# First stage of a hybrid decoder layer on one core: scale row, order of the first loads, and products on zeros

## The chip, the core and the metric

One core of a Trainium2 chip runs the whole kernel in one launch. The metric is the device time of an execution in microseconds (us), from the first to the last instruction; below, the median of three runs. Engines are called by their names: TensorE (products and transposes; PE in the profile, PEld its weight loads), VectorE (DVE), ScalarE (ACT), GpSimd (POOL), and SyncE (SP), which only issues transfers.

## What is computed

The reference is one decoder layer for 512 tokens of width 1024 in float32: a gated feed-forward block of inner width 2816, a mixer (four differential attention heads beside state-space channel groups), and a second feed-forward block. Each is normed before and after. Only the beginning matters here:

```python
def rms_norm(x, g):
    xf = x.astype(jnp.float32)
    y = xf * lax.rsqrt(jnp.mean(xf * xf, axis=-1, keepdims=True) + EPS)
    return (y * g.astype(jnp.float32)).astype(x.dtype)

def swiglu(x, w_gate, w_up, w_down):
    return (jax.nn.silu(x @ w_gate) * (x @ w_up)) @ w_down
...
h = swiglu(rms_norm(x, ff1_pre_g[l]), ff1_w_gate[l], ff1_w_up[l], ff1_w_down[l])
```

## The kernel before

**Tiling.** The 512 tokens are four blocks of 128 (`x_sb[0]` to `x_sb[3]`, L101). A block stands with its tokens on the partitions and its 1024 values along them. `load_x` (L103) fetches a block on SyncE's queue, blocks 0 and 1 in two halves each (L109, L110).

**Norm.** `Normed.tile(t)` (L176) norms a block in two halves of 512 columns. `sum_sq` (L164) has ACT square a half; the sum goes to one column, and the squares themselves, which nobody reads, to a tile called junk, one for the norms in front of a block and one for those behind (L96, L166). `rsqrt_of` (L155) adds the two sums on VectorE (L158) and takes the root on GpSimd (L161). VectorE then multiplies each half by that column and by the scale row (L185). The scale row has to stand on all 128 partitions: `gain_row` (L112) lets GpSimd's queue load it 128 times from memory (L115). TensorE transposes the scaled halves (L190), ACT writes their high part (L193), rounded to the products' number format, and VectorE the rest as a low part (L194).

**Products.** A product of two float32 matrices is three products of high and low parts (`mm3`, L149). `weights` (L136) loads 512 KB of weights on SyncE's queue into one of three raw buffers (L137, L138); ACT writes their high part (L125) and VectorE or GpSimd the low part (L126). The first feed-forward block begins with four such column units, two of w_gate and two of w_up (L994 to L1000): first for the tokens of blocks 0 and 1, which are normed first, then for blocks 2 and 3 (`halves`, L212). Its very first unit takes the low part of the weights last (L216 to L221). After that a column unit is 24 products of 512 columns, and parameter work for the state-space part is drawn in between them (`tick`).

**Order.** The engines' queues aren't written by hand in this stage. A scheduler takes the instructions in the program's order, but lets a later one go ahead on its engine where an earlier one isn't ready; each engine then runs its list in order. A buffer is written again only when its readers are done, and the scheduler adds the waits. What is held by hand is a few instructions that are issued behind others (`after`, `behind`): the parts of the first weights behind the high and low parts of the first tokens (L995), and the squares of blocks 2 and 3 behind those of blocks 0 and 1 (L999).

The layer begins so:

```python
    xn = Normed(ff1_pre_g)
    started = [xn.tile(t) for t in range(NT)]
    for g in started[0:2]:
        next(g)
...
        behind[:] = [normed[0 if n == 0 else 1], normed[2]]
        lead1.append(col_weights(w, f * P))
        if n < 2:
            load_x(2 + n)
            with after(*normed[1:]):
                next(started[n])
```

Of the kernel before, what the change touches and what calls it, by code (L numbers as in the profile page):

```python
# [8 lines left out]
F32 = mybir.dt.float32  # L9
# [7 lines left out]
P = 128  # L17
# [32 lines left out]
def hybrid_layer(  # L50
# [24 lines left out]
    def claim(tl):  # L75
        """Takes the page now, before its first real writer is due."""
        pool.memset(tl[:, 0, 0, 0:1] if len(tl.shape) == 4 else tl[:, 0, 0:1], 0.0)
        return tl
# [7 lines left out]
    def bank(tag="m", name="bank"):  # L86
        return psum.tile([P, 512], F32, tag=tag, name=name, bufs=4 if tag == "acc" else 2)

    # ------------------------------------------------------------------ constants
# [6 lines left out]
    junk = {tag: const.tile([P, 512], BF16, name=f"junk_{tag}") for tag in ("pre", "post")}  # L96
    mhalf = const.tile([P, 1], F32, name="mhalf")
    pool.memset(mhalf, -0.5)

    # ------------------------------------------------------------------ residual stream  # L100
# [8 lines left out]
    load_x(0, 2)  # L109
    load_x(1, 2)  # L110

# [8 lines left out]
    # ------------------------------------------------------------------ exact float32 products  # L120
# [7 lines left out]
    @contextmanager  # L128
    def after(*instructions):
        """What this block puts on the engines of these instructions is issued behind them."""  # L130
        with ExitStack() as order:
            for ins in instructions:
                order.enter_context(tc.issue_after(ins))
            yield

    def weights(src, shape, paged=False):  # L136
        raw = ring.tile(shape, F32, tag="raw", name="raw", bufs=3)  # L137
        sp.dma_start(out=raw, in_=src)  # L138
        if paged:
            both = page([P, 2] + list(shape[1:]), F32R, "w_lead")  # L140
            wh, wl = both[:, 0], both[:, 1]
        else:
            wh = ring.tile(shape, F32R, tag="wh", name="wh")
            wl = ring.tile(shape, F32R, tag="wl", name="wl")
        with after(*behind):
            split(raw, wh, wl, pool if paged else lo_engine[0])
        return wh, wl
# [6 lines left out]
    # ------------------------------------------------------------------ norms  # L154
# [9 lines left out]
    def sum_sq(src, scale, tag):  # L164
        s = tiny(1, f"ss_{tag}", bufs=4)
        into = junk["pre" if tag[:3] == "pre" else "post"][:, 0:src.shape[1]]  # L166
        sum_sq.ins = act.activation(into, src, AF.Square, scale=scale, accum_out=s).ins  # L167
        return s

    class Normed:  # L170
        def __init__(self, gain):
            self.g = gain_row(gain, DM, "pre_g")
            self.hi = [page([P, 4, SEQ], F32R, "xn_hi") for _ in range(2)]
            self.lo = [page([P, 4, SEQ], F32R, "xn_lo") for _ in range(2)]
# [25 lines left out]
    # ------------------------------------------------------------------ projections  # L200
    def col_weights(w, c0, paged=False):
        return weights(w[0, :, c0:c0 + P].rearrange("(k p) c -> p k c", p=P), [P, KD, P], paged)
# [9 lines left out]
    def halves(units, xn, started, late_lo=False):  # L212
        """Four column units, first for the tokens that are normed first."""
        for a in (0, 256):
            for j, (ps, (hi, lo)) in enumerate(units):
                if late_lo and a == j == 0:  # L216
                    for k in range(KD):
                        for n in range(2):
                            pe.matmul(ps[:, 0:256], hi[:, k, :], xn.get(k, 0, 256)[n], start=(k == n == 0), stop=False)
                    for k in range(KD):  # L220
                        pe.matmul(ps[:, 0:256], lo[:, k, :], xn.get(k, 0, 256)[0], start=False, stop=(k == KD - 1))  # L221
                else:
                    col_mm(ps, (hi, lo), xn, a, a + 256)
                if a == 0 and j in (0, 2) and started:
                    for _ in started.pop(0):
                        pass

    def outer(nf, last, ts=range(NT)):
        """Reduction-outer order, the last steps token block by token block."""
        return [(f, t) for f in range(nf - last) for t in ts] + [(f, t) for t in ts for f in range(nf - last, nf)]  # L230
# [69 lines left out]
    # ------------------------------------------------------------------ SwiGLU  # L300
# [39 lines left out]
    # ------------------------------------------------------------------ float32 functions on short rows  # L340
# [92 lines left out]
    # ------------------------------------------------------------------ state-space parameters  # L433
    def cmul_rows(o, a, b):
        """o, a, b: [P, 2, GP] complex rows."""
        t = row(2 * GP).rearrange("p (r g) -> p r g", r=2)
        u = row(2 * GP).rearrange("p (r g) -> p r g", r=2)
        dve.tensor_tensor(t, a, b[:, 0:1, :].broadcast_to([P, 2, GP]), ALU.mult)
        dve.tensor_tensor(u, a, b[:, 1:2, :].broadcast_to([P, 2, GP]), ALU.mult)
        dve.tensor_tensor(o[:, 0, :], t[:, 0, :], u[:, 1, :], ALU.subtract)  # L440
        dve.tensor_tensor(o[:, 1, :], t[:, 1, :], u[:, 0, :], ALU.add)

    def cmul_wide(o_re, o_im, a_re, a_im, f, g0, ng, inner):
        """o = a * f for [P, ng, inner] tiles and per-(partition, group pair) factors f [P, 2, GP]."""
# [17 lines left out]
    def pslot(shape, dtype=F32, name=""):  # L462
        """Next 2 KB slot of the pages that the parameter work owns."""
# [18 lines left out]
    def ssm_small():  # L482
# [50 lines left out]
        # (a_bar - 1) / lam  # L533
# [16 lines left out]
        # skip gains of four groups, on partitions 32 apart, and where they stand among the taps  # L550
# [7 lines left out]
    def ssm_tables():  # L558
        # phases of e^{i theta 8 c}
# [17 lines left out]
        # input and output maps  # L577
# [36 lines left out]
    def ssm_maps(blk):  # L614
        if True:
# [3 lines left out]
            # a^{7-tau} b_bar, transposed to rows (tau, h')  # L619
# [19 lines left out]
            # C a^{t+1}  # L639
# [14 lines left out]
            # C a^j for j = 0 to 8  # L654
# [8 lines left out]
            # Re(C a^j b_bar) and the skip, the rows of the causal block matrix  # L663
# [45 lines left out]
    # ------------------------------------------------------------------ state-space mixer  # L709
# [119 lines left out]
    # ------------------------------------------------------------------ differential attention  # L829
# [17 lines left out]
    def att_query(h, xn):  # L847
        """Scaled queries of the two components, [hi; lo] and [lo; hi] on the partitions."""
# [9 lines left out]
    def att_key(h, xn):  # L858
        """Keys: the high part of each component on both halves, the low parts as they come."""
# [47 lines left out]
    def att_norm(h, i):  # L907
        """One token block of a head's output, normed; yields before the transposes back."""
# [24 lines left out]
    def merged(*streams):  # L933
        """Streams of (length, generator), each kept equally far along."""
# [47 lines left out]
    # ------------------------------------------------------------------ the layer  # L982
    xn = Normed(ff1_pre_g)
# [10 lines left out]
    for n, (f, w) in enumerate((f, w) for f in range(2) for w in (ff1_w_gate, ff1_w_up)):  # L994
        behind[:] = [normed[0 if n == 0 else 1], normed[2]]  # L995
        lead1.append(col_weights(w, f * P))
# [131 lines left out]
```

## Time and profile before

| | |
|---|---|
| three runs, us | 987.87, 988.95, 989.09 |
| median, us | 988.95 |
| span of the profiled execution, us | 988.80 |
| TensorE busy, products | 956.1 us, 97% |
| VectorE, ACT, GpSimd busy | 471.4, 339.4, 157.3 us |
| bytes moved | 107.70 MB, 109 GB/s on the mean |
| granted TensorE clock, mean | 0.990 |

The span of the profiled execution runs from its first to its last instruction. No other time of that execution is given, so it stands for its own time; it is 0.15 us below the median. TensorE is busy nearly always, so its idle time and its clock are what is left. The column of the granted clock has records only from TensorE's first rise on: in the first 20 us it reads 1.00 although the products there run at about half the later pace, so for that stretch the pace itself is to be read.

### The profile page before, as it was taken

To read this page: it belongs to the slowest core of one execution; us is meant where nothing else is said; L and a number is where in the kernel's file an instruction comes from. 1 tells how busy PE (TensorE), PEld (TensorE's weight loads), DVE (VectorE), ACT (ScalarE), POOL (GpSimd) and SP (SyncE) were. 2 spreads that over 40 slices of the span, in tenths; PEclk is the share of its full clock that TensorE was granted. 3 is DMA by queue.
4 is the path that set the end of the run, shared out by engine and by line. 5 is a ranking of instruction groups with operands and counts; after the bars stand their busy time and mean duration, and the time that the engine had idled before them with its cause. 6 is when DMAs were issued, how large, how long until landed. Compare 5 with 4: busy or idle time off the path is not lost.

```text
span 988.8 us, 12741 instructions
## 1 busy us (share of the span) xinstructions
PE 956.1 (97%) x4931; PEld 791.5 (80%) x4931; DVE 471.4 (48%) x946; ACT 339.4 (34%) x567; POOL 157.3 (16%) x216
## 2 busy tenths in 40 slices
PE   5999999999999999998899899999999999999997
PEld 4988777788888888986677677988888888888886
DVE  5599877633331325447467657623333333322323
ACT  5423333323221334222577545522223232312221
POOL 2105333100000033236234315000000000000000
PEclk9999999999999999999899899999999999999999
DMA  7535543533323261596211205322333333232312
GB/s 226 166 92 153 163 131 109 152 97 95 107 86 107 86 192 50 212 195 141 65 43 43 86 23 169 107 64 86 107 87 104 93 99 104 88 107 85 107 43 86
DMA packets 146172, 107.70 MB, mean 109 GB/s; under 512 B 15568, under 2 KB 126704, under 8 KB 145344
## 3 DMA queue, kind: packets, MB, share of 16 engines
q1 hardware_dynamic: 143776, 100.93, 34.8%
q0 software_dynamic: 1184, 3.87, 1.4%
q10 hardware_dynamic: 1152, 2.10, 0.6%
q8 instruction: 39, 0.64, 0.3%
q14 instruction: 21, 0.17, 0.1%
HBM read 97.99 MB, written 8.88 MB: 108 GB/s over the span
## 4 chain that ended last, share of the span: by engine, by line
PE 48%; ACT 1%; DVE 1%; issue 1%; DMA 1%; POOL 0%; DVEq 0%; POOLq 0%; ACTq 0%
PE ps_gu L152 8%; PE ps_gu L150 8%; PE ps_gu L151 8%; PE acc L152 5%; PE acc L150 5%; PE acc L151 5%; PE ps_sc L879 1%; PE ps_o L904 1%; PE ps_sc L878 1%; PE ps_y L776 1%; PE ps_k L150 1%; PE ps_sc L880 1%; DMA raw<-in_ff_w_gate_dram 1%; PE ps_k L151 0%; PE ps_q L150 0%
## 5 line engine op out<-in xcount | busy, mean ns | idle before, releaser
L125 ACT CAST wh<-raw 128x1024 fp32r<-128x1024 f32 x150 | 157.7, 1053 | 448.5 <-issue 152.9
L126 DVE TENSOR_TENSOR wl<-raw,wh 128x1024 fp32r<-128x1024 f32 x132 | 164.1, 1246 | 249.2 <-ACT wh L125 245.1
L150 PE MATMUL ps_gu<-xn_hi,wh 128*128 128x512 f32 (+1 forms) x696 | 265.3, 382 | 0.0
L151 PE MATMUL ps_gu<-xn_lo,wh 128*128 128x512 f32 (+1 forms) x696 | 265.2, 381 | 0.0
L152 PE MATMUL ps_gu<-xn_hi,wl 128*128 128x512 f32 (+1 forms) x696 | 264.9, 381 | 0.0
L150 PEld LDWEIGHTS ps_gu<-xn_hi,wh 128*128 128x128 f32 x696 | 130.8, 188 | 25.4 <-issue 0.8
L152 PEld LDWEIGHTS ps_gu<-xn_hi,wl 128*128 128x128 f32 x696 | 130.8, 188 | 25.0
L151 PEld LDWEIGHTS ps_gu<-xn_lo,wh 128*128 128x128 f32 x696 | 131.0, 188 | 24.7
L150 PE MATMUL acc<-wh,h 128*128 128x512 f32 x352 | 136.9, 389 | 0.0
L151 PE MATMUL acc<-wl,h 128*128 128x512 f32 x352 | 136.9, 389 | 0.0
L152 PE MATMUL acc<-wh,h 128*128 128x512 f32 x352 | 136.1, 389 | 0.0
L319 DVE TENSOR_TENSOR hf<-sg,ps_gu 128x512 f32<-128x512 f32 x44 | 30.2, 686 | 105.8 <-PE ps_gu L152 105.1
L150 PEld LDWEIGHTS acc<-wh,h 128*128 128x128 f32 x352 | 66.1, 188 | 13.8
L152 PEld LDWEIGHTS acc<-wh,h 128*128 128x128 f32 x352 | 66.1, 188 | 13.6
L151 PEld LDWEIGHTS acc<-wl,h 128*128 128x128 f32 x352 | 66.1, 188 | 13.6
L281 POOL TENSOR_SCALAR ss<-ss_post 128x1 f32<-128x1 f32 x12 | 2.6, 213 | 457.8 <-ACT junk_post L167 457.8
L126 POOL TENSOR_TENSOR wl<-raw,wh 128x1024 fp32r<-128x1024 f32 x18 | 44.1, 2456 | 52.8 <-ACT wh L125 52.7
L321 ACT CAST h<-hf 128x512 fp32r<-128x512 f32 x44 | 27.3, 621 | 36.6 <-DVE hf L319 30.0
L322 DVE TENSOR_TENSOR h<-hf,h 128x512 fp32r<-128x512 f32 x44 | 30.1, 684 | 1.4 <-ACT h L321 1.4
L190 PE MATMUL ps_xn<-ident,xs 128*128 128x128 f32 x96 | 14.9, 299 | 13.7 <-DVE xs L185 12.1
L167 ACT ACTIVATE junk_post<-acc 128x512 bf16<-128x512 f32 x24 | 14.3, 596 | 40.1 <-PE acc L152 39.9
L317 ACT ACTIVATE sg<-ps_gu 128x512 f32<-128x512 f32 x44 | 25.8, 587 | 1.5 <-PE ps_gu L152 1.5
(283 smaller groups left out, 1220.4 us busy)
## 6 DMA issues: line engine op xcount, KB each, us to landing
raw<-in_ff_w_gate_dram SPq DMA_DIRECT2D x44, 512.0 KB, 3.9
raw<-in_ff_w_up_dram SPq DMA_DIRECT2D x44, 512.0 KB, 3.9
raw<-in_ff_w_down_dram SPq DMA_DIRECT2D x44, 512.0 KB, 3.3
raw<-in_w_in_dram SPq DMA_DIRECT2D x16, 512.0 KB, 4.1
raw<-in_w_out_dram SPq DMA_DIRECT2D x8, 512.0 KB, 3.3
im_d<-itca SPq DMA_DIRECT2D x4, 512.0 KB, 5.0
om_d<-taps SPq DMA_DIRECT2D x4, 512.0 KB, 3.7
im<-im_d SPq DMA_DIRECT2D x2, 1024.0 KB, 10.2
```

The source lines that it names most:

```text
L125: act.copy(wh, raw)
L126: eng.tensor_tensor(wl, raw, wh.bitcast(F32), ALU.subtract)
L150: pe.matmul(ps, a[0], b[0], start=start, stop=False)
L151: pe.matmul(ps, a[0], b[1], start=False, stop=False)
L152: pe.matmul(ps, a[1], b[0], start=False, stop=stop)
L167: sum_sq.ins = act.activation(into, src, AF.Square, scale=scale, accum_out=s).ins
L190: pe.transpose(ps[:, k * P:(k + 1) * P], xs[h][:, k * P:(k + 1) * P], ident)
L317: act.activation(sg, ps_g, AF.Silu)
L319: dve.tensor_tensor(hf, sg, ps_u, ALU.mult)
L321: act.copy(hi, hf)
L322: dve.tensor_tensor(lo, hf, hi.bitcast(F32), ALU.subtract)
L776: pe.matmul(ps[par * 64:par * 64 + 64, g * 64:(g + 1) * 64], lhs, rhs[:, g, par], start=(g == n == 0), stop=(g == 7 and n == 1), skip_grou ...
```

## The change

- The scale row of the first norm is loaded once, 4 KB into one partition on ACT's queue, and spread over the 128 partitions by two float32 products with a row of ones, whose results ACT copies into the row's tile (half by half).
- The two junk tiles become one. It is set to zero by VectorE, and TensorE begins with 14 products of 128x512 that read this tile for both operands.
- The first and second load of weights wait: a one-column copy on GpSimd writes into their raw buffer, and reads the last column of token block 0 and of block 1. The third and fourth have no such copy.
- Comments and docstrings go.

```diff
-    junk = {tag: const.tile([P, 512], BF16, name=f"junk_{tag}") for tag in ("pre", "post")}
+    junk = const.tile([P, 512], BF16, name="junk")
+    dve.memset(junk, 0.0)
...
+    ones = const.tile([1, P], F32, name="ones")
+    dve.memset(ones, 1.0)
+
+    def warm(n):
+
+        ps = bank(name="ps_warm")
+        for _ in range(n):
+            pe.matmul(ps, junk[:, 0:P], junk, start=True, stop=True)
...
     load_x(0, 2)
+    first_g = gains.tile([P, DM], F32, tag="gain", name="pre_g")
+    act.dma_start(out=first_g[0:1, :], in_=ff1_pre_g[0:1, :])
     load_x(1, 2)
+    warm(14)
+    for h in range(2):
+        cs = slice(h * 512, (h + 1) * 512)
+        ps = bank("acc", "ps_g")
+        pe.matmul(ps, ones, first_g[0:1, cs], start=True, stop=True)
+        act.copy(first_g[:, cs], ps)
...
-    def weights(src, shape, paged=False):
+    def weights(src, shape, paged=False, behind_x=None):
         raw = ring.tile(shape, F32, tag="raw", name="raw", bufs=3)
+        if behind_x is not None:
+            pool.tensor_copy(raw[:, 0, 0:1], behind_x)
         sp.dma_start(out=raw, in_=src)
...
-        into = junk["pre" if tag[:3] == "pre" else "post"][:, 0:src.shape[1]]
+        into = junk[:, 0:src.shape[1]]
...
-        def __init__(self, gain):
-            self.g = gain_row(gain, DM, "pre_g")
+        def __init__(self, gain, g=None):
+            self.g = g if g is not None else gain_row(gain, DM, "pre_g")
...
-    def col_weights(w, c0, paged=False):
-        return weights(w[0, :, c0:c0 + P].rearrange("(k p) c -> p k c", p=P), [P, KD, P], paged)
+    def col_weights(w, c0, paged=False, behind_x=None):
+        return weights(w[0, :, c0:c0 + P].rearrange("(k p) c -> p k c", p=P), [P, KD, P], paged, behind_x)
...
-    xn = Normed(ff1_pre_g)
+    xn = Normed(ff1_pre_g, first_g)
...
-        lead1.append(col_weights(w, f * P))
+        lead1.append(col_weights(w, f * P, behind_x=(x_sb[0][:, DM - 1:DM], x_sb[1][:, DM - 1:DM], None, None)[n]))
```

## Rows read from the trace of the kernel before

**Rows 1.** The page: busy time and share of each engine

```profile
PE 956.1 (97%) x4931; PEld 791.5 (80%) x4931; DVE 471.4 (48%) x946; ACT 339.4 (34%) x567; POOL 157.3 (16%) x216
```

**Rows 2.** Waits of TensorE, 0 to 100 us: us in total, times, longest

```profile
PE ps_xn L190 <- DVE xs L185: 11.4, 2, 10.2
```

**Rows 3.** Windows: length, busy PE, PEld, DVE, ACT, POOL; PEclk, DMA, GB/s

```profile
80.00:100.00 20.00, 20.00 (x92) 16.55 (x91) 19.60 (x53) 5.82 (x7) 9.95 (x16) 1.00 0.65 178
```

**Rows 4.** Timeline, 0 to 25 us: start, us, engine, line, what [idle before]

```profile
0.72 1.28 ACT L167 ACT_TABLE_LOAD   x1 [0.72 <-PEq L1114]
...
3.77 0.63 ACT L167 ACTIVATE junk_pre<-x 128x512 bf16<-128x512 f32 x1 [1.77 <-DMA x<-in_x_dram]
...
5.73 0.56 POOL L161 TENSOR_TENSOR rinv_pre<-rinv_pre,mhalf 128x1 f32<-128x1 f32 x1 [2.30 <-DVE rinv_pre L158]
...
9.37 1.42 DVE L185 SCALAR_TENSOR_TENSOR xs<-x,rinv_pre,pre_g 128x512 f32<-128x512 f32 x2 [3.73 <-DMA pre_g<-in_ff_pre_g_dram]
...
10.95 0.63 ACT L167 ACTIVATE junk_pre<-x 128x512 bf16<-128x512 f32 x1 [1.06 <-DMA x<-in_x_dram]
...
11.48 0.19 ACT L167 ACTIVATION_READ_ACCUMULATOR junk_pre<-x 128x1 f32 x1
...
12.59 1.42 DVE L185 SCALAR_TENSOR_TENSOR xs<-x,rinv_pre,pre_g 128x512 f32<-128x512 f32 x2 [0.67 <-POOL rinv_pre L161]
12.67 1.05 ACT L125 CAST wh<-raw 128x1024 fp32r<-128x1024 f32 x1
...
13.92 1.28 DVE L194 TENSOR_TENSOR xn_lo<-ps_xn,xn_hi 128x512 fp32r<-128x512 f32 x2
...
15.25 1.46 DVE L194 TENSOR_TENSOR xn_lo<-ps_xn,xn_hi 128x512 fp32r<-128x512 f32 x2
...
15.99 0.58 PE L219 MATMUL ps_gu<-xn_lo,wh 128*128 128x256 f32 x1 [0.23 <-DVE xn_lo L194]
```

**Rows 5.** Groups by form on GpSimd: count, busy us, mean ns

```profile
L98 POOL MEMSET mhalf<- 128x1 f32 x1 | 0.1, 98 | 0.0
```

**Rows 6.** Windows of the start; the last two are DMA share, GB/s

```profile
1.50:4.50 3.00, 0.00 (x0) 0.00 (x0) 0.22 (x1) 1.22 (x3) 1.91 (x6) 1.00 0.80 242
...
8.50:11.00 2.50, 0.82 (x4) 0.82 (x5) 1.42 (x2) 0.78 (x3) 0.00 (x0) 1.00 0.94 308
```

**Rows 7.** Timeline of TensorE, 458 to 482 us

```profile
462.33 0.35 PE L878 MATMUL ps_sc<-k,q 128*128 128x256 f32 x1 [3.16 <-DVE tsin L746]
...
477.15 0.63 PE L152 MATMUL ps_q<-xn_hi,wl 128*128 128x512 f32 x1
477.58 0.63 PE L150 MATMUL ps_q<-xn_hi,wh 128*128 128x512 f32 x1
```

**Rows 8.** Timeline of TensorE, 0 to 20 us

```profile
19.35 0.37 PE L150 MATMUL ps_gu<-xn_hi,wh 128*128 128x256 f32 x1
19.56 0.28 PE L151 MATMUL ps_gu<-xn_lo,wh 128*128 128x256 f32 x1
19.68 0.52 PE L221 MATMUL ps_gu<-xn_hi,wl 128*128 128x256 f32 x3
```

**Rows 9.** Timeline of TensorE, 505 to 507.5 us

```profile
505.87 0.83 PE L904 MATMUL ps_o<-v,att 128*128 128x128 f32 x6
```

**Rows 10.** Groups by form on ACT

```profile
L839 ACT COPY v<-acc 128x512 f32<-128x512 f32 x4 | 2.1, 600 | 0.0
```

**Rows 11.** Windows of TensorE: length, busy us, PEclk, DMA, GB/s

```profile
462.00:463.00 1.00, 0.67 (x4) 1.00 0.36 106
...
464.00:465.00 1.00, 1.00 (x15) 0.50 0.00 0
```

**Rows 12.** Timeline of SyncE's issues, 5 to 60 us

```profile
11.43 2.62 SPq L487 DMA_DIRECT2D ldt<-in_ssm_log_dt_dram  x1
14.18 1.76 SPq L554 DMA_DIRECT2D dcol<-in_ssm_d_dram  x4
17.90 0.39 SPq L138 DMA_DIRECT2D raw<-in_ff_w_up_dram  x1
```

## Prediction

> **What bounds the kernel now.** I read the page's busy shares first: TensorE is busy for 97% of the span [rows 1], so time can be won only where it idles or runs at its lower clock. Then its waits in the first 100 us: nearly all of its idle time there, 11.4 us, is two waits of the first transposes (L190) for the normed tokens (L185), the longest 10.2 us [rows 2]. From then on its stream has no hole for a long while (20.00 us busy of 20.00 [rows 3]). Weights, scalings and parameter work behind the start are released by TensorE's own progress through rings of buffers, so I take it that an earlier start moves all of that forward, one for one. The figure to forecast is the moment the product stream becomes steady, 15.99 us [rows 4].
>
> The timeline of the first 16 us shows why it is 15.99 [rows 4]. Engines start at 0.72. The squares of token block 0 start at 3.77, its root ends at 6.29 (5.73 + 0.56), yet its scaling starts only at 9.37: it waits for the scale row that GpSimd loads as 128 copies. That isn't the last wait. The second half of block 1 lands at 10.95; squares, sum and root take until its scaling at 12.59, 1.64 us later. From there to 15.99 are 3.40 us, on VectorE mainly: two scalings (1.42), two low parts of block 0 (1.28 from 13.92), two of block 1 (from 15.25). So the late landing of block 1 sets the start; the scale row alone is hidden behind it.
>
> **The change, part by part.** *Scale row.* 512 KB from the GpSimd queue go away, 4 KB on ACT's queue come; ACT issues it ahead of any square and the 4 KB have until about 6.7 us to land. *Weights behind tokens.* Two one-column copies on GpSimd, about 0.1 us each (nearest: a 128x1 memset, 98 ns [rows 5]), wait for blocks 0 and 1. Behind them on GpSimd stands the root of block 0, due later than both, so they cost nothing there. Without the 512 KB, blocks 0 and 1 (1.05 MB) are the first bytes: 0.73 MB have moved by 4.50 at 242 GB/s, the remaining 0.32 MB take 1.0 to 1.3 us at 308 to 242 GB/s [rows 6], so block 1 lands near 5.8 instead of 10.95, 5.1 us earlier. This cover falls away, and what is late next counts.
>
> *Products on zeros.* This is what is late next. The diff makes one tile, junk, of the two that the squares write to (L166), and the 14 products read that tile. So the first square cannot write before the last zero product has read. Call its end T. A memset of 128x512 on VectorE is not in the trace: 0.1 us (a one-column memset [rows 5]) to 0.71 (one scaling [rows 4]); I take 0.3, near the lower end since it reads nothing, and 0.1 of hand-over: TensorE starts at 1.1. A 512-column product takes 0.43 us at the 1.2 GHz level (477.15 to 477.58) [rows 7], so 14 take 6.0, and with the last one's tail (0.63 - 0.43) T = 7.3. Before, the pitch of 256-column products fell from 0.21 to 0.12 us at 19.56 [rows 8], 3.57 us after the stream became steady. If the zeros do as much, 8 run slowly (3.4 us) and 6 at about 0.22, and T = 6.1. I take the middle, T = 6.7; with the memset's bounds, 5.9 to 7.7.
>
> *Behind T.* ACT computes two squares of block 0; each with its sum takes 0.72 us (10.95 to 11.48 + 0.19 [rows 4]), two about 1.5. The two scale products are float32: a record pair of 128 columns is 0.22 us (six records in 0.83 with the tail, so 0.11 apart) [rows 9], times four for 512 columns, 0.9 us each at 2.4 GHz and about 1.75 at 1.2. At 2.4 they are ready at T+0.9 and T+1.8, and ACT copies each in 0.60 [rows 10]: T+1.5 to T+2.7. Then the squares of block 1, 1.5, to T+4.2; sum and root 0.95 (11.67 to 12.59 before, 0.92). Its scaling starts at T+5.15 = 11.85, against 12.59. Block 0's scaling, at T+2.5, is out of the way. The 3.40 us behind it remain, being VectorE's: the stream is steady at 15.25, 0.74 us earlier.
>
> *Clock.* I count nothing for it behind T. Between the scale products (end near 8.5) and 15.25 TensorE has only sixteen transposes, in two bursts. Later in this kernel a wait of 3.16 us, up to 462.33 [rows 7], is followed by a granted clock of 0.50 (1.2 GHz) at 464 us [rows 11]; here two waits of about two us surround one burst. So the stream probably begins at 1.2 GHz, as before, and pays the same.
>
> *First weights.* SyncE's queue isn't written by hand: before, a small parameter load (ldt) was issued at 11.43, ahead of the fourth weights (17.90), which stand earlier in the program but had to wait [rows 12]. So while the first weights wait for GpSimd's copy, blocks 2 and 3 and the third weights (no copy before them) can go ahead. Up to and with the first weights that is 3.2 MB at most: 2.4 MB after 4.50, at 308 GB/s 7.9 us, so 12.4 [rows 6]. Their high part (1.05 us, [rows 4]) is then there at 13.5, before the stream's 15.25: hidden, with 1.8 us to spare. The second weights, 0.52 MB more, land near 14.1 and are wanted 24 products later: hidden.
>
> **Sum.** 15.99 - 15.25 = 0.74 us less: 988.80 (the profiled span; no other time of that execution is given) becomes 988.06. The span stands 0.15 below the median of the runs, 988.95, so I predict 988.2. Bounds of T alone give 987.4 to 989.2. I take 0.2% (2.0 us) as about what a measurement of this kernel tells from no change; the forecast lies inside.
>
> **Rivals.** *The clock holds (faster).* If TensorE is still at 2.4 GHz at the steady start, 17 products of 256 columns save 0.21 - 0.12 us each [rows 8], 1.6 us; the time is 988.2 - 1.6 = 986.6, and 986.0 if T is 6.1. For it: the transposes keep TensorE partly busy. Against it: the fall at 464 [rows 11]. The Trainium skill (TensorE: Matmul & The Clock Gate, "What's actually happening") speaks for it: the slow clock is the default and "activity releases the throttle", so zeros should do it too; its section "HAM oscillation" speaks against its lasting, since there a wait between bursts brings the slow clock back. Chance 0.28, an unforeseen better order on ACT included.
>
> *The first weights come late (slower).* ACT runs in order, and the high part of the first weights stood ahead of block 1's high parts (12.67 [rows 4]). If they land at G, the stream can start no sooner than G + 1.05 + 0.60 + 0.7 = G + 2.35 (weights' high part, one cast, one low part). That decides from G = 12.9, is slower than before from 13.6 and by over 0.2% from 15.6. At 242 GB/s the 2.4 MB last until 14.4, and the tiny loads (ldt, and dcol, 1.76 us to issue at 14.18 [rows 12]) may go ahead too: G = 16, start 18.35, 991.3. For it: the order of [rows 12]; against: 308 GB/s and more were reached. The Trainium skill (DMA: Bandwidth & Descriptors, "HWDGE ordering") says that each DMA engine takes a queue's descriptors in ring order; by this the weights asked for last do come last, which would make it likelier, and no row here tests it. Chance 0.18.
>
> *Zeros do not lift the clock (no change).* Then T = 7.3, the scale products end at T+3.5, the last copy at T+4.1, block 1's scaling is at T+6.55 = 13.85 and the stream at 17.25: 1.26 us later, 990.2. Chance 0.08.
>
> **Numbers.** Forecast 0.46, clock 0.28, late weights 0.18, idle zeros 0.08. So faster 0.28, same 0.46 + 0.08 = 0.54, slower 0.18. The forecast's own range is 987.4 to 989.2; the range for 8 in 10 goes to the fast end of the clock case, 985.9, and past the idle zeros into the late weights, 990.9.
>
> **What would show it.** Right: the first square starts at the end of the zero products, near 6.7, though block 0 has landed before 5; block 1's scaling near 11.9; the steady stream near 15.3 with 0.21 us between products at first. Wrong: squares that start at 3.8 (no wait on junk: the start then moves by some 3 us and the forecast fails on the fast side); products 0.12 us apart from the start (clock); ACT waiting for the weights' load ahead of block 1's high parts (late weights); or a TensorE hole behind 20 us that wasn't there.

## The result, and the profile after

The changed kernel takes 995.03 us (median of five runs, 993.0 to 995.36); the kernel before takes 988.95 (five runs of the same chip, 987.87 to 992.15). The ratio is 1.0056, 95% interval 1.0038 to 1.0074: **slower by 0.56%**, where 988.2 and no change were forecast. The profiled execution has a span of 993.2 us and a time of 995.03, so 1.8 us lie outside the span; that was so in every later run with both numbers. So a span doesn't stand for a time: the profiled execution of before, with its span of 988.80, took about 990.6 us (an estimate by the same 1.8), which is 1.6 above its median and not 0.15 below it. The two profiles lie 4.45 us apart and the medians 6.1 (the ratio, over all runs, is 5.5 us); what the profiles below explain is the 4.45. Line numbers are now 19 higher than before.

The page's first part, after; [rows 1] answer to it. TensorE has 18 records more (the 14 products on zeros and the scale row's two products, four records), and is just as full:

```profile
PE 962.9 (97%) x4949; PEld 794.6 (80%) x4949; DVE 470.8 (47%) x948; ACT 341.2 (34%) x569; POOL 158.3 (16%) x217
```

TensorE's waits over the whole span, after (in all, times, longest). Of the first line's 5.4 us, 4.5 lie in the start (two waits, 3.3 and 1.2), where before it were 11.4 [rows 2]: TensorE is busy with zeros for much of the rest. The second line has grown from 0.2 us.

```profile
PE ps_xn L209 <- DVE xs L204: 5.4, 3, 3.3
PE ps_u L169 <- ACT xn_hi L212: 4.3, 1, 4.3
...
PE ps_it L654 <- DVE itca L469: 1.8, 1, 1.8
PE ps_warm L107 <- DVE junk L97: 1.2, 1, 1.2
```

The line that answers to the second, in the same list of before:

```profile
PE ps_u L150 <- ACT xn_hi L193: 0.2, 1, 0.2
```

Where the time goes can be read from the start of the first product of each stage in both timelines (us, one profiled execution each):

| first product of | before | after | later by |
|---|---|---|---|
| the first column units (ps_gu) | 15.18 | 16.61 | 1.43 |
| the 27th product of them | 20.64 | 21.16 | 0.52 |
| the 1001st (parameter work lies before it) | 237.72 | 238.97 | 1.25 |
| the mixer's first projection (ps_u) | 393.66 | 399.31 | 5.65 |
| attention's products with the values (ps_o) | 486.11 | 492.02 | 5.91 |
| attention's output (o_att) | 575.78 | 580.11 | 4.33 |
| end of the last instruction | 988.80 | 993.25 | 4.45 |

So the start costs half a microsecond, and **4.4 us are lost at one place, 380 us behind everything that the change edits on purpose**: between the first feed-forward block and the mixer.

**The start.** Timeline of the changed kernel, 0 to 20 us (start, us, engine, line, what, idle before and its releaser); [rows 4] answer to it:

```profile
1.18 5.25 PE L107 MATMUL ps_warm<-junk 128*128 128x512 bf16 x14 [1.18 <-DVE junk L97]
...
6.46 0.63 ACT L186 ACTIVATE junk<-x 128x512 bf16<-128x512 f32 x1 [1.57 <-PE ps_warm L107]
...
9.07 0.23 DVE L863 TENSOR_SCALAR subln<-subln 128x128 f32<-128x128 f32 x1 [7.34 <-DMA subln<-in_attn_subln_g_dram]
9.22 0.21 DVE L177 TENSOR_SCALAR rinv_pre<-ss_pre,ss_pre 128x1 f32<-128x1 f32 x1
9.48 0.63 ACT L186 ACTIVATE junk<-x 128x512 bf16<-128x512 f32 x1 [1.07 <-DMA x<-in_x_dram]
...
10.10 0.18 POOL L156 COPY raw<-x 128x1 f32<-128x1 f32 x1 [5.51 <-DMA x<-in_x_dram]
...
10.24 0.56 POOL L180 TENSOR_TENSOR rinv_pre<-rinv_pre,mhalf 128x1 f32<-128x1 f32 x1
...
10.84 1.41 DVE L204 SCALAR_TENSOR_TENSOR xs<-x,rinv_pre,pre_g 128x512 f32<-128x512 f32 x2 [1.42 <-POOL rinv_pre L180]
...
13.42 0.69 DVE L213 TENSOR_TENSOR xn_lo<-ps_xn,xn_hi 128x512 fp32r<-128x512 f32 x1 [1.04 <-ACT xn_hi L212]
...
14.03 1.40 DVE L204 SCALAR_TENSOR_TENSOR xs<-x,rinv_pre,pre_g 128x512 f32<-128x512 f32 x2
14.41 1.05 ACT L142 CAST wh<-raw 128x1024 fp32r<-128x1024 f32 x1 [0.18 <-DMA raw<-in_ff_w_gate_dram]
...
17.34 0.58 PE L238 MATMUL ps_gu<-xn_lo,wh 128*128 128x256 f32 x1
```

The first square waits for the last product on zeros (6.46). Block 1 lands at 9.5 and 10.1 (its square, and GpSimd's copy that reads its last column). VectorE stands for 7.34 us at the scaling of a small row for attention, subln, whose load is late; block 0's sum stands behind it. GpSimd stands for block 1 at its second copy, and block 0's root behind that. So block 0 is scaled at 10.84 instead of 9.37, block 1 at 14.03 instead of 12.59, behind a low part of block 0, and the stream is steady at 17.34 instead of 15.99.

Windows of the same stretch (length; busy PE, PEld, DVE, ACT, POOL; PEclk, DMA share, GB/s): between 4.5 and 6.5 us the transfers fall to less than half of what they are on either side (113 GB/s), with no 512 KB of copies in the way any more. And the clock is down in the last row; it had risen during the zeros, whose last four stand 0.22 us apart and the others 0.43.

```profile
1.50:4.50 3.00, 3.00 (x8) 1.06 (x7) 0.23 (x1) 0.89 (x1) 1.39 (x5) 1.00 0.87 237
4.50:6.50 2.00, 2.00 (x8) 0.74 (x7) 0.00 (x0) 0.43 (x2) 0.09 (x1) 1.00 0.69 113
6.50:8.50 2.00, 1.83 (x4) 0.51 (x4) 0.00 (x0) 1.88 (x5) 0.00 (x0) 1.00 0.74 265
8.50:11.00 2.50, 0.00 (x0) 0.00 (x0) 0.51 (x3) 1.52 (x4) 0.71 (x2) 0.56 1.03 375
```

**The mixer's doorstep.** Here the first block's result is normed and added to the residual x (squares of acc, junk_post before), and the new x is normed for the mixer (squares of x, junk_pre before). ACT's timeline, before, 378 to 402 us:

```profile
380.71 0.63 ACT L167 ACTIVATE junk_pre<-x 128x512 bf16<-128x512 f32 x1 [1.79 <-DVE x L288]
...
381.34 0.58 ACT L167 ACTIVATE junk_post<-acc 128x512 bf16<-128x512 f32 x1
...
381.91 0.62 ACT L167 ACTIVATE junk_pre<-x 128x512 bf16<-128x512 f32 x1
...
386.62 0.60 ACT L167 ACTIVATE junk_post<-acc 128x512 bf16<-128x512 f32 x1 [1.37 <-PE acc L152]
```

The same view, after:

```profile
382.01 0.63 ACT L186 ACTIVATE junk<-x 128x512 bf16<-128x512 f32 x1 [1.85 <-DVE x L307]
...
382.77 0.63 ACT L186 ACTIVATE junk<-x 128x512 bf16<-128x512 f32 x1
...
383.52 0.60 ACT L186 ACTIVATE junk<-acc 128x512 bf16<-128x512 f32 x1
...
388.64 0.60 ACT L186 ACTIVATE junk<-acc 128x512 bf16<-128x512 f32 x1
...
396.51 0.63 ACT L186 ACTIVATE junk<-x 128x512 bf16<-128x512 f32 x1 [3.98 <-DVE x L307]
```

Before, the square of the next acc stands *between* the two squares of x: the two write different tiles, so the scheduler may swap them. After, all write one tile, each is ordered behind the one ahead of it in the program, and the square of acc stands behind both. It comes 2.2 us later than before (383.52 against 381.34), of which 1.2 are the whole kernel's lag and 0.9 the order's. VectorE's list changes with it. Before, the sum of block 1's new x (L288, 382.92) stood ahead of block 0's scalings (384.25); after, it stands behind them (386.30 against 384.97), so block 1's scalings start at 390.09 instead of 386.44. VectorE's timeline, before:

```profile
382.92 0.75 DVE L288 SCALAR_TENSOR_TENSOR x<-half,rinv_post,x 128x512 f32<-128x512 f32 x1
...
384.25 1.41 DVE L185 SCALAR_TENSOR_TENSOR xs<-x,rinv_pre,pre_g 128x512 f32<-128x512 f32 x2
...
386.44 1.41 DVE L185 SCALAR_TENSOR_TENSOR xs<-x,rinv_pre,pre_g 128x512 f32<-128x512 f32 x2 [0.66 <-POOL rinv_pre L161]
...
388.64 0.75 DVE L288 SCALAR_TENSOR_TENSOR x<-half,rinv_post,x 128x512 f32<-128x512 f32 x1
```

The same view, after. At 390 us the scalings meet something:

```profile
384.97 1.41 DVE L204 SCALAR_TENSOR_TENSOR xs<-x,rinv_pre,pre_g 128x512 f32<-128x512 f32 x2
386.30 0.75 DVE L307 SCALAR_TENSOR_TENSOR x<-half,rinv_post,x 128x512 f32<-128x512 f32 x1
...
390.09 3.56 DVE L204 SCALAR_TENSOR_TENSOR xs<-x,rinv_pre,pre_g 128x512 f32<-128x512 f32 x2
393.57 2.84 DVE L307 SCALAR_TENSOR_TENSOR x<-half,rinv_post,x 128x512 f32<-128x512 f32 x1
```

and in GpSimd's, after and then before:

```profile
390.35 5.52 POOL L143 TENSOR_TENSOR wl<-raw,wh 128x1024 fp32r<-128x1024 f32 x2
```

```profile
389.11 4.91 POOL L126 TENSOR_TENSOR wl<-raw,wh 128x1024 fp32r<-128x1024 f32 x2 [0.50 <-ACT wh L125]
```

Two scalings take 3.56 us instead of 1.41, and the step behind them, which makes block 2's new x (L307), 2.84 instead of 0.75: both now fall beside GpSimd's low parts of the mixer's weights. By the trace's single records, which the line merges, the first of the two scalings, which began before the low parts, took 0.74 us; the second took 2.90, so it and the step behind it were each held by 2.1 to 2.2 us, together the size of TensorE's wait. Before, block 2's x was done at 390.06, 0.95 us after those had begun (389.11). ACT waits 3.98 us for that x, and TensorE 4.27 for an ACT that stands there. That GpSimd's low parts are what holds the two is read from these times; no run took them out of the way. TensorE's timeline, after:

```profile
399.31 1.01 PE L169 MATMUL ps_u<-xn_hi,w_lead 128*128 128x256 f32 x3 [4.27 <-ACT xn_hi L212]
```

The windows show the second price of such a hole: the granted clock falls behind it. After:

```profile
395.00:400.00 5.00, 0.73 (x4) 0.69 (x3) 4.19 (x7) 3.49 (x9) 2.63 (x2) 0.79 0.51 175
400.00:405.00 5.00, 5.00 (x26) 4.99 (x26) 4.06 (x8) 1.77 (x5) 1.63 (x3) 0.53 0.35 108
```

Before, for the same ten microseconds:

```profile
395.00:400.00 5.00, 3.93 (x34) 3.69 (x32) 5.00 (x2) 1.72 (x3) 4.53 (x2) 1.00 1.02 414
400.00:405.00 5.00, 4.54 (x38) 4.57 (x39) 3.86 (x8) 2.04 (x5) 0.56 (x2) 1.00 1.00 403
```

The projections then take as long as before (27.1 us from the first to the last ps_u in both), since before they had waits of their own; so the loss is the wait, 4.3 of the 4.4 us. Of the 5.9 us at 486 us, 1.6 come back in attention: before has two stretches at half clock there, near 552 and 562 us, after only one, near 558.

### The profile page after: what moved, and what is told of

Same layout as the page of the kernel before. It is cut to its first block, busy times and chain, and to the rows that moved or that the text cites. A ratio compares the mean times of both kernels' runs of the same rounds, so it can differ in the third digit from the quotient of the medians.

```text
span 993.2 us, 12798 instructions
## 1 busy us (share of the span) xinstructions
PE 962.9 (97%) x4949; PEld 794.6 (80%) x4949; DVE 470.8 (47%) x948; ACT 341.2 (34%) x569; POOL 158.3 (16%) x217
## 4 chain that ended last, share of the span: by engine, by line
PE 48%; DVE 2%; ACT 1%; POOL 1%; issue 1%; DMA 1%; POOLq 0%; DVEq 0%; ACTq 0%
PE ps_gu L170 8%; PE ps_gu L171 8%; PE ps_gu L169 8%; PE acc L169 5%; PE acc L170 5%; PE acc L171 5%; PE ps_sc L898 1%; PE ps_o L923 1%; PE ps_y L795 1%; PE ps_sc L897 1%; PE ps_k L169 1%; DMA raw<-in_ff_w_gate_dram 1%; PE ps_sc L899 1%; PE ps_k L170 0%; PE ps_q L169 0%
## 5 line engine op out<-in xcount | busy, mean ns | idle before, releaser
L186 ACT ACTIVATE junk<-acc 128x512 bf16<-128x512 f32 x24 | 14.3, 597 | 38.8 <-PE acc L171 38.5
L902 ACT ACTIVATE att<-ps_sc,mx 128x128 f32<-128x128 f32 (+3 forms) x32 | 16.8, 526 | 19.8 <-DVE mx L901 19.3
```

The lines of the kernel that those rows point to most:

```text
L902: act.activation(pg[:, c, 0:n], ps[:, 0:n], AF.Exp, bias=mx, accum_out=ssum[:, c:c + 1])
```

## The experiments

Theory A: one junk tile for all squares fixes their order on ACT, and that costs 4 to 5 us at the mixer. Theory B: the squares' wait on the zero products, and so the late start, costs it. All ratios are to the kernel before on the same chip, over all runs. (e1's own expectation has another rival as B, that any changed start shifts the scheduler's whole order; in e9's, A and B are theories of the loads.)

**e1: the kernel before with one junk tile.**

```diff
-    junk = {tag: const.tile([P, 512], BF16, name=f"junk_{tag}") for tag in ("pre", "post")}
+    junk = const.tile([P, 512], BF16, name="junk")
...
-        into = junk["pre" if tag[:3] == "pre" else "post"][:, 0:src.shape[1]]
+        into = junk[:, 0:src.shape[1]]
```

> The kernel before, with one tile instead of two for the squares that nobody reads, and nothing else of the change. Theory A (one tile puts all of ACT's squares in the program's order, and at the handover to the mixer that costs): the start stays at 15.99, TensorE waits some 4 us for the high part of a normed block ahead of the mixer's first products (0.2 before), and the time is 3.5 to 6 us above before. Theory B (the changed start shifts the scheduler's whole order, and any changed start would do it): no difference from before, within 2 us.

Measured: 992.79 us, ratio 1.0045 (1.0029 to 1.0061). TensorE's waits, 380 to 405 us:

```profile
PE ps_u L150 <- ACT xn_hi L193: 4.3, 1, 4.3
```

None of the change's loads, copies or zeros is in it, and it has the same wait; VectorE's two groups are there with 3.55 and 2.84 us. In its profiled execution the first ps_u is 4.5 us later than before, with no lag (0.1 us at the 1001st product) ahead of it. That is A; and since nothing of the start was edited, a changed start isn't needed for the wait. One thing was not as expected: the steady stream came at 15.26 us, not at 15.99. The start's code is that of before, so two executions can lie 0.7 us apart there, and smaller differences between the starts below tell nothing by themselves.

**e2: the change with two junk tiles** (zeros and ones in scratch buffers, for which there is room).

```diff
-    junk = const.tile([P, 512], BF16, name="junk")
-    dve.memset(junk, 0.0)
+    zeros = tmp.tile([P, 512], BF16, tag="scratch", name="zeros")
+    dve.memset(zeros, 0.0)
+    junk = {tag: const.tile([P, 512], BF16, name=f"junk_{tag}") for tag in ("pre", "post")}
...
-            pe.matmul(ps, junk[:, 0:P], junk, start=True, stop=True)
+            pe.matmul(ps, zeros[:, 0:P], zeros, start=True, stop=True)
...
```

> The changed kernel with two tiles for the squares as before, and the zeros (and the row of ones) in buffers of their own. Theory A: the wait of 4.3 us ahead of the mixer's first products falls to 0.2 to 0.5, and 4 to 5 us come back there; the squares of block 0 start when it has landed, near 4, instead of 6.46. The steady start is still set by block 1's landing near 10 us: 15 to 16.5. In all 987.5 to 990. Theory B: the wait at the mixer stays, 991 or more.

Measured: 989.42 us, 1.0014 (0.9998 to 1.003). The wait of ps_u is gone. With e1 this is the effect both ways.

**e3: the change with the zeros in a tile of their own, but still one junk tile** (as e2, with the one tile kept).

> The changed kernel with the zeros (and the row of ones) in buffers of their own, but still one tile for all squares. It undoes the wait of the first squares on the zero products alone. Theory A: the start is as in the run with two tiles (15 to 16.5), the wait at the mixer stays at about 4 us, and the time is 992 to 995, 4 to 5 us above the run with two tiles. If the wait on the zeros were what cost, it would be as fast as that run.

Measured: 992.97 us, 1.0044 (1.0028 to 1.006). The first square starts at 3.52 us, not 6.46, and the wait of 4.3 us at ps_u is there: the early squares don't help.

**e5: the change with two junk tiles, the zeros in one of them**, so that only the wait on the zero products is left.

```diff
+    junk = {tag: const.tile([P, 512], BF16, name=f"junk_{tag}") for tag in ("pre", "post")}
+    dve.memset(junk["pre"], 0.0)
...
+            pe.matmul(ps, junk["pre"][:, 0:P], junk["pre"], start=True, stop=True)
...
```

> The whole change, but with two junk tiles again, and the zeros in the one for the pre-norm squares. So the squares still wait for the zero products (to about 6.4 us), but pre- and post-norm squares may stand in either order on ACT's list. If the one tile's order is the cost (theory A), the wait of ps_u for ACT's high part falls from 4.3 us to under 0.5 and the time falls to that of the two-tile kernel within 1 us: 988.5 to 990.5. If the wait of the first squares on the zero products is a cost of its own (theory B), steady start and time stay above the two-tile kernel: 991 to 993, with first products of the stream 1 us or more later than there.

Measured: 989.43 us, 1.0009 (0.9996 to 1.0022), although the first square starts at 6.88 us. In TensorE's waits, 380 to 405 us, stands only what stood there before the change:

```profile
PE ps_xn L209 <- DVE rinv_post L177: 1.6, 1, 1.6
```

B falls. The four kernels with one tile (the change, e1, e3, and e14 below) lie at 1.0044 to 1.006, the eleven with two at 0.9985 to 1.0014, with none in between.

**e4, e6, e7, e8: the parts of the change by themselves**, all with two junk tiles. e4 is e2 without `warm(14)`; e6 is e4 without the copies on GpSimd, so that only the scale row is left; e7 has the zeros alone; e8 is e2 without the copies.

```diff
-    warm(14)
...
-        lead1.append(col_weights(w, f * P, behind_x=(x_sb[0][:, DM - 1:DM], x_sb[1][:, DM - 1:DM], None, None)[n]))
+        lead1.append(col_weights(w, f * P))
...
```

> The run with two tiles without the 14 products on zeros. If the zeros give the clock nothing at the steady start (it falls again behind the scale products), this is the same as the run with two tiles within 1.5 us, and the transposes and the first products run at the slow pace in both. If they do help, it is slower by 1.5 to 3 us.

> Two junk tiles, no zero products, no one-column copies on GpSimd: of the change only the scale row (4 KB, spread by two products) is left. If the copies on GpSimd cost something (they stand ahead of block 0's root), the first scaling comes earlier than in the two-tile kernel without zeros, and the time is 0.5 to 1.5 us below it: 987.5 to 988.5. If they only reorder the loads, so that without them the weights compete with the tokens, block 1 lands later by 1 to 2 us and the time is as before the change or up to 1 us above: 988 to 990.

> Two junk tiles, the 14 zero products, but the scale row loaded as 128 copies from GpSimd and no one-column copies there. If zeros help by a higher clock at the start of the stream, the time falls by up to 1.6 us below the kernel before: 986.5 to 988.5. If TensorE has lost the higher clock by the time its stream is steady (idle from about 7 to 16 us), the steady start and the time are those of before within 0.5 us.

> The two-tile kernel (zeros, scale row and all) without the one-column copies on GpSimd. If those copies cost by standing ahead of block 0's root, which waits on GpSimd for block 1's landing, the first scaling comes 0.5 to 1.5 us earlier and the time is below the two-tile kernel by about as much, 988 to 989. If block 1 lands later without them, because the first two weights are requested before it is through, block 1's second half lands 1 to 2 us later and the time is 989.5 to 991.

| | steady stream from, us | time, us | ratio |
|---|---|---|---|
| e2 all of it | 17.17 | 989.42 | 1.0014 (0.9998 to 1.003) |
| e8 without copies | 15.87 | 990.0 | 1.0011 (0.9998 to 1.0025) |
| e7 zeros alone | 15.90 | 989.35 | 1.0006 (0.9994 to 1.0018) |
| e4 without zeros | 15.41 | 988.91 | 1.0005 (0.9995 to 1.0015) |
| e6 scale row alone | 14.59 | 988.3 | 1.0004 (0.999 to 1.0017) |

The second column is the start of the row that stands last in [rows 4]. Each part is without an effect that can be told. The zeros alone leave the start where it was, as their second case said. The copies' price can't be told either: e8's stream starts 1.3 us before that of e2, e6's 0.8 before that of e4, and the times of each two can't be told apart. Against e4's expectation, the first products of e2 and e4 stand 0.12 us apart in both, at the higher clock. In e4 and e6 the second half of block 1 is squared at 8.8 and 8.6 us, in none of the five at 5.8; so what holds it is something else.

**e9 to e12: what holds the start.** The base is e4. e9 holds the loads of blocks 2 and 3 behind block 1. e10 loads blocks 0 and 1 in one request each. e11 takes the load of the row subln out of the start. e12 is e11 with ACT's copies of the scale row ahead of the squares of block 1.

```diff
+            pool.tensor_copy(x_sb[2 + n][:, 0:1], x_sb[1][:, DM - 1:DM])
             load_x(2 + n)
...
-    load_x(0, 2)
+    load_x(0, 1)
...
-    load_x(1, 2)
+    load_x(1, 1)
...
-        pool.dma_start(out=A.sub, in_=attn_subln_g[0:1, :].broadcast_to([P, VD]))
+        with after(*pool_behind):
+            pool.dma_start(out=A.sub, in_=attn_subln_g[0:1, :].broadcast_to([P, VD]))
...
+    for g, ahead in zip(started[0:2], ([], first_copies)):
+        with after(*ahead):
+            next(g)
...
```

> Base: the two-tile kernel without zero products (its block 1 lands by 8.8 us). Two more one-column copies on GpSimd hold the loads of blocks 2 and 3 until block 1 has landed. If the bytes of blocks 2 and 3 are what keeps block 1 (theory A), its second half lands near 6 us and its first square starts below 6.5. If block 1's packets come slowly by themselves between 4.5 and 8 us, with the DMA engines mostly idle (theory B), it lands at 8 or later all the same, and the stream becomes steady no earlier than in the base, 14.9 us, or later since the weights and blocks 2 and 3 are asked for later. Time by A 987 to 988, by B 988.5 to 990.5.

> Base as in the run before, but blocks 0 and 1 are loaded in one request each: rows of 4 KB instead of two of 2 KB, so 256 packets for them and not 512. If the slow stretch comes by the number of packets asked for (it begins after about 350 of the 512 in the runs so far), block 1 is through by 6 us. If it comes by time (from about 4.9 us), the last third of block 1 again lands after 7 us. The first square of block 0 waits for the whole block, so it starts later, near 4.5. Time within 1.5 us of the base either way: 987.5 to 990.5.

> Base as in the runs before, but the small row of the attention norm (64 KB as 128 copies, asked for at 1.7 us on GpSimd's queue) is loaded behind the last root so far, out of the start. Then VectorE's scaling of that row, which waited for it until about 8 us, no longer stands ahead of block 0's sum: the sum follows block 0's squares at 5 to 6 us, not at 8 or later. If these 64 KB also make the slow stretch of the DMA engines from 4.9 us, block 1's second half lands by 7 us, otherwise at 8 to 9. Steady stream 0 to 1 us earlier than the base's 14.9; time 987 to 990.

> As the run before, and ACT copies the spread scale row ahead of the squares of block 1 (an order given by hand), so that block 0 can be scaled before block 1 has landed: first scaling near 7 us instead of 9 to 10, first transposes near 8. If VectorE's four scalings and four low parts (5.7 us) set the steady start, it comes 1 to 2 us earlier than the base's, at 13 to 14 us. If block 1's landing at 8 to 9 us sets it, it comes at about 14. What is gained at the start is worth at most 2 us in the end, and waits for the parameter work on VectorE at 100 to 180 us take part of it back (1 us or more in four of the runs so far): time 986 to 988.5, against 988 to 989 for the kernel before. Under 986 would say that nothing is taken back.

Measured: e9 987.94 us, 0.9996 (0.9983 to 1.0009); e10 988.79, 1.0004 (0.999 to 1.0017); e11 988.64, 1.0002 (0.9987 to 1.0018); e12 989.67, 1.0012 (0.9997 to 1.0027). In e9 the first half of block 1 is squared at 7.27 (7.37 in e4) and not below 6.5, while the second lands 0.9 us earlier than in e4: blocks 2 and 3 have a part in it at most. (The expectations call the base's stream steady from 14.9 us; by the table's measure it is 15.41, and e9's 14.35.) In e10 block 1 is through at 6.0, so whole rows help it, but the scaling of subln then waits until 9.46 and holds block 0's scaling, and the stream is steady at 15.25. In e11 the transfers between 4.5 and 6.5 us run at 347 GB/s (112 in e4), the first half is squared at 5.55, block 0 is scaled at 6.83; but the second half, at 7.97, missed the 7 that was expected. So the small row is the brake, and what was then late was the third thing, the first weights: ACT makes their high part ahead of block 1's. ACT's timeline in e11:

```profile
12.52 1.04 ACT L142 CAST wh<-raw 128x1024 fp32r<-128x1024 f32 x1 [0.77 <-DMA raw<-in_ff_w_gate_dram]
```

and in e12, where ACT is through with block 0's high parts by 10.14 (11.75 in e11), and whose time was outside what was expected:

```profile
12.79 1.04 ACT L143 CAST wh<-raw 128x1024 fp32r<-128x1024 f32 x1 [2.65 <-DMA raw<-in_ff_w_gate_dram]
```

The streams follow at 14.82 and 15.10 us, 2.3 us behind the cast in both. The clock differed, too, and nothing here says why: e12's products stay 0.21 us apart until 21 us, those of e11 are 0.12 apart from 15.05 on.

**e13: all three late things at once**: subln later, the first three weights right behind blocks 0 and 1 (no copies into raw buffers), blocks 2 and 3 held behind block 1.

> Two junk tiles, scale row spread by products, no zero products, the small row of the attention norm loaded later, the first three weights asked for right behind blocks 0 and 1, and blocks 2 and 3 held behind block 1 (two one-column copies on GpSimd). If the first weights were what ended last in e11 (they landed at 12.5 us there), they land near 9 to 10, block 1 by 8, and the steady stream starts at 12.5 to 13.8 us, against 15.99 before. If an early start reaches the end one for one, the time falls by 2 to 3 us: 985.5 to 986.8. If the parameter work on VectorE takes back 1 to 2 us between 90 and 180 us, as it did in e4, e6 and e11, the time is 987 to 988, the same as before.

Measured: 986.86 us (985.07 to 989.13) against 988.64, ratio 0.9985 (0.9969 to 1.0001). Its start, from the timelines of ACT and TensorE:

```profile
10.94 1.05 ACT L142 CAST wh<-raw 128x1024 fp32r<-128x1024 f32 x1
...
13.25 0.58 PE L238 MATMUL ps_gu<-xn_lo,wh 128*128 128x256 f32 x1
```

The stream is steady 2.74 us earlier than before, no wait for weights is left ahead of it, and the median falls by 1.8 us. It is faster than the changed kernel by 0.7%; from the kernel before it can't be told quite, by its interval. In the profiled execution its lead is 2.38 us at the 27th product, 1.25 at the 1001st and 2.24 at the end.

**e14: the changed kernel itself, with only subln's load later.** One tile and zeros are as in the change; the edit is e11's.

> The changed kernel as it is, one junk tile and zero products included; only the small row of the attention norm (64 KB) is loaded behind the last root so far. If that row is what delayed the start (it slowed block 1's packets and its scaling stood ahead of block 0's sum), block 1's second half lands at 8 us or before, block 0's first scaling starts by 9.3 us (it was 10.84) and the steady stream comes at 15 to 16 us, not 17.34. If not, it stays at 17 or later. The time stays over that of before either way, since the one tile still orders the squares: 991 to 994.

Measured: 994.07 us, just above what was expected, 1.006 (1.0039 to 1.008). Windows of its start, same columns as above:

```profile
4.50:6.50 2.00, 2.00 (x7) 0.69 (x5) 0.00 (x0) 0.37 (x1) 0.18 (x1) 1.00 0.90 270
6.50:8.50 2.00, 2.00 (x5) 0.66 (x4) 0.21 (x1) 1.73 (x5) 0.18 (x1) 1.00 0.89 313
```

270 GB/s where the changed kernel has 113. GpSimd's copy behind block 1 runs at 7.62 (10.10 before this edit), block 0 is scaled at 9.13 (10.84), the stream is steady at 15.63 (17.34): in this pair of executions, 64 KB of a row that nobody needs for another 480 us, with its scaling, made the start 1.7 us later. And since the one tile is still there, the time hasn't moved by an amount that can be told.

## Why the prediction was wrong

**The step that failed** is the price of the merged tile. The prediction saw that one tile ties the first squares to the zeros (T), counted it there, and put it at nothing everywhere else: work behind the start, it took, is "released by TensorE's own progress", so that a shift of the start goes through one for one. It never asked who else writes that tile: 24 squares of x on one side, 24 of acc and 20 within the mixer on the other, and between the two sides the two tiles had left the order free. This term is missing in the sum; it measures 4.3 to 4.5 us, and e1, e2, e3 and e5 show it on both sides. "A TensorE hole behind 20 us that wasn't there" was named as what would show the forecast wrong, and it is what showed it.

**T was right**, in part by luck. The memset took 0.27 us (0.3 forecast), the products 5.25, T = 6.43 (6.7), the first square came at 6.46. But ten products ran slowly and not eight; that the middle between two cases was taken made up for it. The scale products took 1.98 us at the higher clock (1.8).

**The start** was forecast 0.74 us earlier and came 1.35 later, by the next two points. **Block 1's landing was wrong**: 5.8 forecast, 9.5 and 10.1 (its two halves) measured. The mean rate of [rows 6] was carried into a stretch that has a rate of its own: 113 GB/s. The cause is of the kind that the change took away: a load of 128 copies of one row on GpSimd's queue. 512 KB of it went, 64 KB stayed, and e14 shows what they do. Before, the same window moves 268 GB/s, but by the packets of the trace 0.40 of its 0.54 MB are copies of rows on GpSimd's queue, and block 1 waits. The Trainium skill (DMA: Bandwidth & Descriptors, "Issuing engines are not separate DMA queues") says that transfers from all issuing engines run on the same 16 DMA engines and interleave; e14 agrees, 113 to 270 GB/s by a load on another queue.

**"They cost nothing there"**, of GpSimd's copies: block 0's root, due when its sum ended (9.43), started at 10.24 behind the second copy, 0.8 us (a copy itself takes 0.18, forecast 0.1). The scaling of subln, which the prediction didn't see, cost the sum another 1.3 (the squares were summed at 7.94, the sum started at 9.22). Before, the same instruction ran at 15.12, behind all four scalings.

**The clock** went as the main case said: up during the zeros, down before the stream (0.56 and 0.50), and the stream began at 1.2 GHz, 0.21 us apart until 19.00. Two things were not foreseen: the rise came 1.7 us behind the steady start, not 3.57, so of the 1.35 us of late start only 0.52 were left at the 27th product; and whether the stream begins at the higher clock doesn't go by the zeros. Of the seven kernels with zeros it does in three (e2, e3, e8), of the nine without in four (e4, e9, e10, e11), by one profiled execution each. So "the clock holds" is no effect of the zeros, and that the change itself began at 1.2 GHz may be chance. The Trainium skill's two rules weighed there (TensorE: Matmul & The Clock Gate, "What's actually happening" and "HAM oscillation") both agree with the change's trace: the clock rose during the zeros and fell in the idle stretch behind them.

**"The first weights come late"** had the right mechanism and the wrong place. In the change the weights landed at 14.4 (12.4 forecast), only 0.18 us too late, since the tokens were later still. Its formula, steady = landing + 2.35, gives 14.87 and 15.14 for e11 and e12; 14.82 and 15.10 were measured.

**"One for one"** is not right at the start either, but less can be said. Through e2 and e4 to e13 the time, by its ratio, falls by about 0.66 us for each microsecond of earlier steady stream (a line through the eleven; correlation 0.87; without e13 it is 0.47, and 0.77). Part of most leads goes between 88 and 240 us, where TensorE waits for parameter work on VectorE (L469): 1.2 us before, 1.7 to 2.9 in the profiled executions of e4 to e13 (ps_it in the list of waits). But e7, with a lead of 0.3 us at the 27th product, loses 1.0 us on the way to the 1001st as well, and e1, whose start is that of before, 1.4; so whether leads are given back or the profiled execution of before was a lucky one in that stretch is open.

The range (985.9 to 990.9) failed to hold 995 because every rival sat in the first 25 us.

## What to carry to other kernels

A tile that only takes in results nobody reads still orders its writers: before merging two such tiles, list every writer in the whole program and ask which pairs the scheduler had swapped. When a transfer is taken out, look for others of its kind in the same stretch, however small, and for what stands behind the instruction that waits for them on its engine's list. Once one late input is early, the next one decides: here the scale row, block 1, the small row and the first weights came due close behind each other, and even the version that moved all of them (e13) gained no more than 0.15%, which isn't quite told from nothing.

## What the runs showed of the hardware

- **A small load of copies slows others far beyond its size**: 64 KB asked for on GpSimd's queue. In seven kernels that have this load in the start (the change, e2 to e6, e8) the window from 4.5 to 6.5 us moves 87 to 153 GB/s, and the second half of block 1 lands at 8.6 to 10.1 us; in the four without it there (e11 to e14) it is 270 to 347 GB/s, and 7.2 to 8.0. (e9, which holds blocks 2 and 3 back, lies between, with 215 and 7.9.) The packets of the trace show the load as 16 of 4 KB, which took 0.94 us each on the mean in the change, between 4.5 and 8.6 us, and 0.22 in e14, where they come at 24 us. Why they are slow is open. In e10 the slow stretch came later: 383 GB/s from 4.5 to 6.5 us, with blocks 0 and 1 through by then, and 109 in the two behind; the small row's scaling came at 9.46.
- **VectorE's steps with two operands in SBUF are held by GpSimd's low parts**: by the single records before and after, all six that began together with such a low part or while it ran (394.56, 397.46 and 604.89 before; 390.75, 393.57 and 609.21 after) took 2.84 to 2.97 us instead of 0.75 and ended 0.54 to 0.55 us behind that low part's end. One that began 0.26 us ahead of it (390.09 after) took 0.74. Before has such holds, too (two scalings in 5.75 us at 394.56), but TensorE didn't stand behind them. Low parts on VectorE that read one operand from PSUM were not held: three in 1.89 us at 392.61 before, beside GpSimd's. The Trainium skill (SBUF — State Buffer, "Who interferes with whom") says just this: a VectorE instruction with two SBUF inputs contends with a GpSimd instruction that reads SBUF, one with at most one SBUF input, outside VectorE's 2-port modes, doesn't. So 0.9 us of order on ACT became 4.3 on TensorE.
- **The moment of the clock's rise isn't set by the zeros**: without them the pace went to 0.12 us per 256 columns from the first products on in e4 and e11, and only at 21 us in e12; with them it fell before the stream and rose again between 14 and 20 us.
